# Row-wise argmax on one core: the last four tiles in column pieces, the last two looked up on VectorE, the last stored from its partitions

## The chip, the cores and the metric

The kernel runs on one core of one Trainium2 chip. The metric is device time in microseconds (us). All runs named here are of state fast, the granted clock was 1.00 in every profile, and nearly all executions of one kernel agree within about 0.1%. Engines: VectorE is DVE in the profile, GpSimd is POOL, ScalarE is ACT, TensorE is PE, SyncE is SP. A "q" behind a name (SPq, POOLq) marks what only that engine's sequencer does. In every profile the time of that execution is 1.8 us more than its span (the prediction reckons with 1.9, the difference of the median and the span).

## The reference

```python
def setup_inputs():
    return {"x": np.random.randn(8192, 8192).astype(np.float32)}

def reference(x):
    return np.argmax(x, axis=1)
```

## The kernel before

There are 64 tiles of 128 rows. Each row of 8192 numbers is 64 chunks of 128. A tile is loaded (4 MB), VectorE takes the maximum of each chunk (`cm`), and then the row's argmax is looked up in two steps: which chunk holds the row maximum (`k`), and where in that chunk it is (`k2`); for the second step the chunk is gathered again from DRAM with an indirect DMA that GpSimd issues. The matches (equal to the maximum, times a descending ramp) are on GpSimd. Lookups are made for groups of four tiles, and the three steps of a group are deferred so that they fall between the maxima of later tiles. Below, the *keys* of tiles are the VectorE step that reads `k` and so releases their gathers; their *finish* is the last step, which writes the result into `res`.

```python
    groups = [4] * 15 + [2, 1, 1]
    ...
    def store(t0, n):
        ps = ppool.tile([n, P], F32, tag="ps")
        nc.tensor.transpose(ps, res[:, t0:t0 + n], ident)
        o = spool.tile([n, P, 2], I32, tag="o")
        nc.gpsimd.memset(o, 0)
        nc.scalar.copy(out=o[:, :, 0:1], in_=ps.unsqueeze(2))
        keep(nc.sync.dma_start(out=out_i32[t0:t0 + n, :], in_=...))

    def stage2(t0, g, cm, now):
        mx = ...                                       # row maximum, VectorE
        w, k = first_match(cm, mx, descC, C, g, "c")   # GpSimd
        def stage3():
            keep(nc.vector.reduce_max(out=k, in_=w, axis=AX.X))
            ...                                        # idx, VectorE
            for i in range(g):
                keep(nc.gpsimd.indirect_dma_start(out=ga[:, i, :], ...))
            w2, k2 = first_match(ga, mx, descL, L, g, "l")   # GpSimd
            def stage4():
                ...                                    # three VectorE steps into res
                if t0 + g == 60:
                    store(0, 60)
            defer(now + 4, stage4)
        defer(now + 1, stage3)

    t = 0
    for g in groups:
        ...
        for i in range(g):
            ...
            parts = 4 if t == NT - 1 else 1            # the last tile in four pieces
            ...                                        # loads (SP queue), then maxima
            run_due(t)
            t += 1
        stage2(t0, g, cm, t - 1)
    run_due(0, all_=True)
    while pending:
        run_due(0, all_=True)
    store(60, NT - 60)
```

Of the kernel before, what the change touches and what calls it, by code (L numbers as in the profile page):

```python
# [1 line left out]

# [4 lines left out]

F32 = mybir.dt.float32
U32 = mybir.dt.uint32
I32 = mybir.dt.int32  # L10
ALU = mybir.AluOpType
AX = mybir.AxisListType


@with_exitstack
def kernel(
    ctx: ExitStack,
    tc: tile.TileContext,
    x: bass.AP,
    out: bass.AP,  # L20
):
    nc = tc.nc
    keep = tc.keep_in_program_order
    N, M = x.shape
    P = 128
    C = 64
    L = M // C
    NT = N // P

    xpool = ctx.enter_context(tc.tile_pool(name="x_sbuf", bufs=5))  # L30
    spool = ctx.enter_context(tc.tile_pool(name="small", bufs=3))
    cpool = ctx.enter_context(tc.tile_pool(name="const", bufs=1))
    ppool = ctx.enter_context(tc.tile_pool(name="psum", bufs=2, space=bass.MemoryType.PSUM))

    oth = out.tensor
    oth2 = type(oth)(name=oth.name, shape=[NT, 2 * P], dtype=I32, base_partition=oth.base_partition)
    out_i32 = oth2.ap()
    x_flat = x.tensor.reshape([N * C, L]).ap()


    descC = cpool.tile([P, C], F32)
    nc.gpsimd.iota(out=descC, pattern=[[-1, C]], base=C, channel_multiplier=0,  # L42
                   allow_small_or_imprecise_dtypes=True)
    descL = cpool.tile([P, L], F32)
    nc.gpsimd.iota(out=descL, pattern=[[-1, L]], base=L, channel_multiplier=0,  # L45
                   allow_small_or_imprecise_dtypes=True)

    base = cpool.tile([P, NT], F32)
    nc.gpsimd.iota(out=base, pattern=[[P * C, NT]], base=C, channel_multiplier=C,  # L49
                   allow_small_or_imprecise_dtypes=True)  # L50

    ident = cpool.tile([P, P], F32)
    nc.gpsimd.iota(out=ident, pattern=[[1, P]], base=0, channel_multiplier=-1,  # L53
                   allow_small_or_imprecise_dtypes=True)
    keep(nc.gpsimd.tensor_scalar(out=ident, in0=ident, scalar1=0.0, scalar2=None, op0=ALU.is_equal))  # L55

    res = cpool.tile([P, NT], F32)

    def first_match(vals, mx, desc, n, g, name):

        w = spool.tile([P, g, n], F32, tag=f"w_{name}")
        for i in range(g):
            keep(nc.gpsimd.tensor_scalar(out=w[:, i, :], in0=vals[:, i, :], scalar1=mx[:, i:i + 1],  # L63
                                    scalar2=None, op0=ALU.is_equal))
            keep(nc.gpsimd.tensor_tensor(out=w[:, i, :], in0=w[:, i, :], in1=desc, op=ALU.mult))  # L65
        k = spool.tile([P, g], F32, tag=f"k_{name}")
        return w, k

    groups = [4] * 15 + [2, 1, 1]
    assert sum(groups) == NT  # L70


    pending = []

    def run_due(now, all_=False):
        while pending and (all_ or pending[0][0] <= now):
            pending.pop(0)[1]()

    def defer(due, fn):
        pending.append((due, fn))  # L80
        pending.sort(key=lambda e: e[0])

    def store(t0, n):
        ps = ppool.tile([n, P], F32, tag="ps")
        nc.tensor.transpose(ps, res[:, t0:t0 + n], ident)  # L85
        o = spool.tile([n, P, 2], I32, tag="o")
        nc.gpsimd.memset(o, 0)  # L87
        nc.scalar.copy(out=o[:, :, 0:1], in_=ps.unsqueeze(2))  # L88
        keep(nc.sync.dma_start(out=out_i32[t0:t0 + n, :], in_=o.rearrange("t p two -> t (p two)")))

    def stage2(t0, g, cm, now):
        mx = spool.tile([P, g], F32, tag="mx")
        keep(nc.vector.reduce_max(out=mx, in_=cm, axis=AX.X))  # L93
        w, k = first_match(cm, mx, descC, C, g, "c")

        def stage3():
            keep(nc.vector.reduce_max(out=k, in_=w, axis=AX.X))  # L97
            idx = spool.tile([P, g], U32, tag="idx")
            keep(nc.vector.tensor_tensor(out=idx, in0=base[:, t0:t0 + g], in1=k, op=ALU.subtract))  # L99
            ga = spool.tile([P, g, L], F32, tag="ga")  # L100
            for i in range(g):
                keep(nc.gpsimd.indirect_dma_start(  # L102
                    out=ga[:, i, :], out_offset=None, in_=x_flat[:, :],
                    in_offset=bass.IndirectOffsetOnAxis(ap=idx[:, i:i + 1], axis=0)))
            w2, k2 = first_match(ga, mx, descL, L, g, "l")

            def stage4():
                keep(nc.vector.reduce_max(out=k2, in_=w2, axis=AX.X))  # L108

                keep(nc.vector.scalar_tensor_tensor(out=res[:, t0:t0 + g], in0=k, scalar=float(L),  # L110
                                               in1=k2, op0=ALU.mult, op1=ALU.add))
                keep(nc.vector.tensor_scalar(out=res[:, t0:t0 + g], in0=res[:, t0:t0 + g],  # L112
                                        scalar1=-1.0, scalar2=float(C * L + L),
                                        op0=ALU.mult, op1=ALU.add))
                if t0 + g == 60:
                    store(0, 60)

            defer(now + 4, stage4)

        defer(now + 1, stage3)  # L120

    t = 0
    for g in groups:
        cm = spool.tile([P, g, C], F32, tag="cm")
        t0 = t
        for i in range(g):
            xt = xpool.tile([P, M], F32, tag="xt")
            parts = 4 if t == NT - 1 else 1
            w = M // parts
            cw = C // parts  # L130
            for q in range(parts):
                keep(nc.sync.dma_start(out=xt[:, q * w:(q + 1) * w],  # L132
                                  in_=x[t * P:(t + 1) * P, q * w:(q + 1) * w]))
            for q in range(parts):
                keep(nc.vector.reduce_max(  # L135
                    out=cm[:, i, q * cw:(q + 1) * cw],
                    in_=xt[:, q * w:(q + 1) * w].rearrange("p (c l) -> p c l", c=cw), axis=AX.X))
            run_due(t)
            t += 1
        now = t - 1  # L140
        stage2(t0, g, cm, now)
    run_due(0, all_=True)
    while pending:
        run_due(0, all_=True)
    store(60, NT - 60)


# [1 line left out]
_INS = ['x']  # L149
_OUTS = [((8192,), 'int64')]  # L150


# [23 lines left out]
```

## Time and profile before

| | before |
|---|---|
| time, median of the rounds with the change | 667.21 us (667.04 to 667.47) |
| span of the profile | 665.3 us |
| VectorE busy, GpSimd busy | 584.1 us (88%), 179.7 us (27%) |
| last packet of the input (DMA records of the trace) | 639.76 us |
| end of tile 63's last maximum | 648.08 us |

The page of the kernel before, the span in 40 slices of 16.6 us; busy tenths, and GB/s moved.

```profile
DVE  2899898998989899898998989899898998989891
...
DMA  9999999999999999999999999999999999999930
GB/s 378 441 428 425 424 441 426 426 431 420 439 426 428 426 426 440 423 430 420 430 423 442 431 418 430 425 440 418 430 431 426 439 421 430 428 426 439 405 161 12
```

The DMA engines are full (9 tenths; 418 to 442 GB/s from the second slice to the 37th) up to the last two slices. The kernel is bound by the stream of its input for some 640 us; only what comes after can be saved by other work on the tail.

The timeline of the kernel before from 599 us on (start us, length us, engine, line, operation, tiles; in brackets the idle time before it and what ended it).

```profile
599.63 8.69 DVE L135 TENSOR_REDUCE cm<-xt 128x64 f32<-128x8192 f32 x1 [1.28 <-DMA xt<-in_x_dram]
...
609.55 8.68 DVE L135 TENSOR_REDUCE cm<-xt 128x64 f32<-128x8192 f32 x1
...
619.02 1.04 POOL L102 DMA_INDIRECT ga<-in_x_dram,idx  x1 [5.99 <-DVE idx L99]
619.05 8.69 DVE L135 TENSOR_REDUCE cm<-xt 128x64 f32<-128x8192 f32 x1 [0.31 <-DMA xt<-in_x_dram]
...
626.79 0.62 POOL L63 TENSOR_SCALAR w<-ga,mx 128x128 f32<-128x128 f32 x1 [2.97 <-DMA ga<-in_x_dram,idx]
...
630.11 8.69 DVE L135 TENSOR_REDUCE cm<-xt 128x64 f32<-128x8192 f32 x1 [2.05 <-DMA xt<-in_x_dram]
...
639.23 8.85 DVE L135 TENSOR_REDUCE cm<-xt 128x16 f32<-128x2048 f32 x4
...
649.93 1.05 POOL L102 DMA_INDIRECT ga<-in_x_dram,idx  x1 [4.57 <-DVE mx L93]
...
655.27 1.04 POOL L102 DMA_INDIRECT ga<-in_x_dram,idx  x1 [0.73 <-DVE idx L99]
...
658.70 0.45 POOL L65 TENSOR_TENSOR w<-w,descL 128x128 f32<-128x128 f32 x1
...
660.38 0.26 ACT L88 CAST o<-ps 4x128 int32<-4x128 f32 x1 [10.47 <-PE ps L85]
```

Tiles 59 to 63 are the five maxima. VectorE begins a whole tile only when all of it has landed (its waits of 1.28, 0.31 and 2.05 us above end with the landing), so it ends it at least 8.7 us after that: it runs about one tile behind the stream. After tile 63 (648.08) the gather of tile 62 (649.93) and the gather of tile 63 (655.27) stand one after the other.

### The profile page before, as it was taken

The page shows a single profiled execution, that of the slowest core. Times are in us where ns is not written, and L with a number is a line of the kernel's source. Part 1 is how long each engine was busy: PE and PEld are TensorE (multiplying, and loading weights), DVE is VectorE, ACT ScalarE, POOL GpSimd, SP SyncE. Part 2 cuts the span into 40 slices and gives each one's busy share as a digit, 9 for nine tenths or more (in the row PEclk, how much of TensorE's full clock was granted, in tenths as well). Part 3 has the DMA queues.
Part 4 walks back from the last instruction along what each step waited for, and adds up shares of the span by engine and source line. Part 5 has one row for each costly group of instructions (what it writes and reads, how often), then busy time and mean ns, then how long its engine had stood idle before and what let it go on. Part 6 is the DMA issues. An engine that isn't in the chain of part 4 may idle for free.

```text
span 665.3 us, 723 instructions
## 1 busy us (share of the span) xinstructions
PE 0.8 (0%) x2; PEld 0.2 (0%) x2; DVE 584.1 (88%) x175; ACT 1.8 (0%) x3; POOL 179.7 (27%) x331
## 2 busy tenths in 40 slices
PE   0000000000000000000000000000000000000000
PEld 0000000000000000000000000000000000000000
DVE  2899898998989899898998989899898998989891
ACT  0000000000000000000000000000000000000000
POOL 1004214041231304214032231304214131331442
DMA  9999999999999999999999999999999999999930
GB/s 378 441 428 425 424 441 426 426 431 420 439 426 428 426 426 440 423 430 420 430 423 442 431 418 430 425 440 418 430 431 426 439 421 430 428 426 439 405 161 12
DMA packets 11786, 272.75 MB, mean 410 GB/s; under 512 B 2116, under 2 KB 2180, under 8 KB 3204
## 3 DMA queue, kind: packets, MB, share of 16 engines
q1 hardware_dynamic: 9731, 268.51, 94.5%
q0 software_dynamic: 2048, 4.20, 1.7%
q14 instruction: 7, 0.05, 0.0%
HBM read 272.63 MB, written 0.07 MB: 410 GB/s over the span
## 4 chain that ended last, share of the span: by engine, by line
DMA 76%; DVE 19%; issue 3%; POOL 0%; SPq 0%; POOLq 0%; PE 0%; ACT 0%; DVEq 0%; ACTq 0%
DMA xt<-in_x_dram 75%; DVE cm L135 18%; DMA ga<-in_x_dram,idx 1%; DVE k L108 0%; SPq L132 0%; POOL w L63 0%; DVE mx L93 0%; DVE k L97 0%; DVE res L110 0%; POOL w L65 0%; DVE res L112 0%; POOLq L171 0%; DVE idx L99 0%; PE ps L85 0%; ACT o L88 0%
## 5 line engine op out<-in xcount | busy, mean ns | idle before, releaser
L135 DVE TENSOR_REDUCE cm<-xt 128x64 f32<-128x8192 f32 (+1 forms) x67 | 555.9, 8301 | 65.9 <-DMA xt<-in_x_dram 65.9
L63 POOL TENSOR_SCALAR w<-cm,mx 128x64 f32<-128x64 f32 x64 | 28.2, 441 | 261.4 <-DVE mx L93 261.4
L102 POOL DMA_INDIRECT ga<-in_x_dram,idx x64 | 62.4, 974 | 115.0 <-DVE idx L99 91.2
L63 POOL TENSOR_SCALAR w<-ga,mx 128x128 f32<-128x128 f32 x64 | 38.8, 606 | 91.7 <-DMA ga<-in_x_dram,idx 91.7
L65 POOL TENSOR_TENSOR w<-w,descL 128x128 f32<-128x128 f32 x64 | 29.1, 454 | 5.3
L65 POOL TENSOR_TENSOR w<-w,descC 128x64 f32<-128x64 f32 x64 | 20.4, 319 | 5.3
L108 DVE TENSOR_REDUCE k<-w 128x4 f32<-128x512 f32 (+2 forms) x18 | 11.1, 617 | 2.9 <-POOL w L65 2.9
L97 DVE TENSOR_REDUCE k<-w 128x4 f32<-128x256 f32 (+2 forms) x18 | 6.8, 379 | 4.8 <-POOL w L65 4.8
L93 DVE TENSOR_REDUCE mx<-cm 128x4 f32<-128x256 f32 (+2 forms) x18 | 6.9, 382 | 0.1
L99 DVE TENSOR_TENSOR idx<-base,k 128x4 uint32<-128x4 f32 (+2 forms) x18 | 2.9, 162 | 0.9 <-DVE k L97 0.3
L112 DVE TENSOR_SCALAR res<-res 128x4 f32<-128x4 f32 (+2 forms) x18 | 3.0, 168 | 0.6
L110 DVE SCALAR_TENSOR_TENSOR res<-k 128x4 f32<-128x4 f32 (+2 forms) x18 | 2.9, 162 | 0.6
L88 ACT CAST o<-ps 60x128 int32<-60x128 f32 (+1 forms) x2 | 0.5, 263 | 658.1 <-PE ps L85 658.1
L85 PE MATMUL ps<-ident,res 128*60 128x128 f32 (+1 forms) x2 | 0.8, 382 | 659.5 <-DVE k L97 649.2
L88 ACT ACT_TABLE_LOAD x1 | 1.3, 1283 | 0.7 <-PEq L160 0.7
L87 POOL MEMSET o<- 60x256 int32 (+1 forms) x2 | 0.6, 301 | 0.0
L55 POOL TENSOR_SCALAR ident<-ident 128x128 f32<-128x128 f32 x1 | 0.5, 534 | 0.0
L85 PEld LDWEIGHTS ps<-ident,res 128*60 128x60 f32 (+1 forms) x2 | 0.2, 104 | 659.8 <-issue 649.2
L42 POOL IOTA descC<- 128x64 f32 x1 | 0.2, 175 | 0.4 <-POOLq L160 0.4
L45 POOL IOTA descL<- 128x128 f32 x1 | 0.2, 228 | 0.0
L53 POOL IOTA ident<- 128x128 f32 x1 | 0.2, 228 | 0.0
L49 POOL IOTA base<- 128x64 f32 x1 | 0.2, 174 | 0.0
(4 smaller groups left out, 0.4 us busy)
## 6 DMA issues: line engine op xcount, KB each, us to landing
xt<-in_x_dram SPq DMA_DIRECT2D x63, 4096.0 KB, 41.0
xt<-in_x_dram SPq DMA_DIRECT2D x4, 1024.0 KB, 37.5
ga<-in_x_dram,idx POOLq DMA_INDIRECT x64, 8.6
out_dram<-o SPq DMA_DIRECT2D x1, 60.0 KB, 1.6
out_dram<-o SPq DMA_DIRECT2D x1, 4.0 KB
```

The lines of the kernel that those rows point to most:

```text
L63: keep(nc.gpsimd.tensor_scalar(out=w[:, i, :], in0=vals[:, i, :], scalar1=mx[:, i:i + 1], scalar2=None, op0=ALU.is_equal))
L65: keep(nc.gpsimd.tensor_tensor(out=w[:, i, :], in0=w[:, i, :], in1=desc, op=ALU.mult))
L85: nc.tensor.transpose(ps, res[:, t0:t0 + n], ident)
L88: nc.scalar.copy(out=o[:, :, 0:1], in_=ps.unsqueeze(2))
L93: keep(nc.vector.reduce_max(out=mx, in_=cm, axis=AX.X))
L97: keep(nc.vector.reduce_max(out=k, in_=w, axis=AX.X))
L99: keep(nc.vector.tensor_tensor(out=idx, in0=base[:, t0:t0 + g], in1=k, op=ALU.subtract))
L102: keep(nc.gpsimd.indirect_dma_start(out=ga[:, i, :], out_offset=None, in_=x_flat[:, :], in_offset=bass.IndirectOffsetOnAxis(ap=idx[:, i:i ...
L108: keep(nc.vector.reduce_max(out=k2, in_=w2, axis=AX.X))
L110: keep(nc.vector.scalar_tensor_tensor(out=res[:, t0:t0 + g], in0=k, scalar=float(L), in1=k2, op0=ALU.mult, op1=ALU.add))
L112: keep(nc.vector.tensor_scalar(out=res[:, t0:t0 + g], in0=res[:, t0:t0 + g], scalar1=-1.0, scalar2=float(C * L + L), op0=ALU.mult, op1=ALU ...
L135: keep(nc.vector.reduce_max(out=cm[:, i, q * cw:(q + 1) * cw], in_=xt[:, q * w:(q + 1) * w].rearrange("p (c l) -> p c l", c=cw), axis=AX.X))
```

## The change

The intent is to shorten the tail: tiles 60 to 63 are loaded and maximized in pieces, so that VectorE can follow the stream; the deferred lookups are counted in pieces, so that they fall between them; tiles 62 and 63 are looked up by VectorE's own max and index instructions, without GpSimd's matches; and tile 63's result goes to DRAM from its 128 partitions, 8 bytes each, without transpose and copy. The first store moves to ScalarE's queue, and the groups' finish comes one tile earlier. The diff, cut to its core:

```diff
-    groups = [4] * 15 + [2, 1, 1]
+    def load_reduce(t, cm, widths):
+        ...                                  # one load per piece, then one maximum per piece
+            step[0] = t * 4 + at // 2048
+            run_due()
...
     def store(t0, n):
...
-        keep(nc.sync.dma_start(out=out_i32[t0:t0 + n, :], ...))
+        keep(nc.scalar.dma_start(out=out_rows[t0:t0 + n, :], ...))
...
-            defer(now + 4, stage4)
-        defer(now + 1, stage3)
+            defer(match_after, finish)
+        defer(gather_after, gather)
+
+    def direct_begin(t, cm):
+        keep(nc.vector.max(out=m8, in_=cm))
+        keep(nc.vector.max_index(out=c8, in_max=m8, in_values=cm))
+        keep(nc.vector.tensor_tensor(out=idx, in0=c8[:, 0:1], in1=base[:, t:t + 1], op=ALU.add))
+        keep(nc.gpsimd.indirect_dma_start(out=ga, ...))
+        return m8, c8, ga
+
+    def direct_end(m8, c8, ga, dst):
+        keep(nc.vector.max_index(out=l8, in_max=m8, in_values=ga))
+        keep(nc.vector.scalar_tensor_tensor(out=dst, in0=c8[:, 0:1], scalar=float(L), ...))
...
+    for g in [4] * 15 + [2]:
...
+            load_reduce(t, cm[:, i, :], [M] if t < 60 else [2048] * 4)
...
+        if g == 4:
+            lookup(t0, g, cm, 4, 7)
+        else:
+            lookup(t0, g, cm, 1, 100)
+
+    load_reduce(62, cm62, [2048] * 4)
+    d62 = direct_begin(62, cm62)
+    load_reduce(63, cm63, [2048] * 3 + [1024, 512, 512])
+    d63 = direct_begin(63, cm63)
+    step[0] = 1000
+    run_due()
+    direct_end(*d62, res[:, 62:63])
+    store(60, 3)
+    direct_end(*d63, o_last[:, 0:1])
+    nc.sync.dma_start(out=out_pairs[63 * P:, :], in_=o_last)
```

More of the change, by code (lines that the diff above doesn't have):

```diff
@@ L35, with out_view @@
     oth = out.tensor
-    oth2 = type(oth)(name=oth.name, shape=[NT, 2 * P], dtype=I32, base_partition=oth.base_partition)
-    out_i32 = oth2.ap()
+    def out_view(shape):
+        return type(oth)(name=oth.name, shape=shape, dtype=I32, base_partition=oth.base_partition).ap()
+    out_rows = out_view([NT, 2 * P])
+    out_pairs = out_view([N, 2])
     x_flat = x.tensor.reshape([N * C, L]).ap()
@@ L48 @@
     base = cpool.tile([P, NT], F32)
-    nc.gpsimd.iota(out=base, pattern=[[P * C, NT]], base=C, channel_multiplier=C,
+    nc.gpsimd.iota(out=base, pattern=[[P * C, NT]], base=0, channel_multiplier=C,
+                   allow_small_or_imprecise_dtypes=True)
+    baseC = cpool.tile([P, NT], F32)
+    nc.gpsimd.iota(out=baseC, pattern=[[P * C, NT]], base=C, channel_multiplier=C,
                    allow_small_or_imprecise_dtypes=True)
@@ L57, with defer, run_due, match @@
     res = cpool.tile([P, NT], F32)
-    def first_match(vals, mx, desc, n, g, name):
-        w = spool.tile([P, g, n], F32, tag=f"w_{name}")
+    o_last = cpool.tile([P, 2], I32)
+    nc.gpsimd.memset(o_last, 0)
+    pending = []
+    step = [0]
+    def defer(steps, fn):
+        pending.append((step[0] + steps, fn))
+        pending.sort(key=lambda e: e[0])
+    def run_due():
+        while pending and pending[0][0] <= step[0]:
+            pending.pop(0)[1]()
+    def load_reduce(t, cm, widths):
+        assert sum(widths) == M
+        xt = xpool.tile([P, M], F32, tag="xt")
+        at = 0
+        for w in widths:
+            keep(nc.sync.dma_start(out=xt[:, at:at + w], in_=x[t * P:(t + 1) * P, at:at + w]))
+            at += w
+        at = 0
+        for w in widths:
+            c0, c1 = at // L, (at + w) // L
+            keep(nc.vector.reduce_max(
+                out=cm[:, c0:c1], in_=xt[:, at:at + w].rearrange("p (c l) -> p c l", l=L), axis=AX.X))
+            at += w
+            step[0] = t * 4 + at // 2048
+            run_due()
+    def match(w, vals, mx, desc, g):
         for i in range(g):
             keep(nc.gpsimd.tensor_scalar(out=w[:, i, :], in0=vals[:, i, :], scalar1=mx[:, i:i + 1],
-                                    scalar2=None, op0=ALU.is_equal))
+                                         scalar2=None, op0=ALU.is_equal))
             keep(nc.gpsimd.tensor_tensor(out=w[:, i, :], in0=w[:, i, :], in1=desc, op=ALU.mult))
-        k = spool.tile([P, g], F32, tag=f"k_{name}")
-        return w, k
-    groups = [4] * 15 + [2, 1, 1]
-    assert sum(groups) == NT
-    pending = []
-    def run_due(now, all_=False):
-        while pending and (all_ or pending[0][0] <= now):
-            pending.pop(0)[1]()
-    def defer(due, fn):
-        pending.append((due, fn))
-        pending.sort(key=lambda e: e[0])
     def store(t0, n):
@@ L85, in store, with lookup, gather @@
         nc.tensor.transpose(ps, res[:, t0:t0 + n], ident)
-        o = spool.tile([n, P, 2], I32, tag="o")
+        o = cpool.tile([n, P, 2], I32, tag=f"o{t0}")
         nc.gpsimd.memset(o, 0)
-        nc.scalar.copy(out=o[:, :, 0:1], in_=ps.unsqueeze(2))
-        keep(nc.sync.dma_start(out=out_i32[t0:t0 + n, :], in_=o.rearrange("t p two -> t (p two)")))
-    def stage2(t0, g, cm, now):
+        keep(nc.scalar.copy(out=o[:, :, 0:1], in_=ps.unsqueeze(2)))
+        keep(nc.scalar.dma_start(out=out_rows[t0:t0 + n, :], in_=o.rearrange("t p two -> t (p two)")))
+    def lookup(t0, g, cm, gather_after, match_after):
         mx = spool.tile([P, g], F32, tag="mx")
         keep(nc.vector.reduce_max(out=mx, in_=cm, axis=AX.X))
-        w, k = first_match(cm, mx, descC, C, g, "c")
-        def stage3():
-            keep(nc.vector.reduce_max(out=k, in_=w, axis=AX.X))
+        wc = spool.tile([P, g, C], F32, tag="wc")
+        match(wc, cm, mx, descC, g)
+        k = spool.tile([P, g], F32, tag="k")
+        def gather():
+            keep(nc.vector.reduce_max(out=k, in_=wc, axis=AX.X))
             idx = spool.tile([P, g], U32, tag="idx")
-            keep(nc.vector.tensor_tensor(out=idx, in0=base[:, t0:t0 + g], in1=k, op=ALU.subtract))
+            keep(nc.vector.tensor_tensor(out=idx, in0=baseC[:, t0:t0 + g], in1=k, op=ALU.subtract))
             ga = spool.tile([P, g, L], F32, tag="ga")
@@ L104, in stage3 @@
                     in_offset=bass.IndirectOffsetOnAxis(ap=idx[:, i:i + 1], axis=0)))
-            w2, k2 = first_match(ga, mx, descL, L, g, "l")
-            def stage4():
-                keep(nc.vector.reduce_max(out=k2, in_=w2, axis=AX.X))
-                keep(nc.vector.scalar_tensor_tensor(out=res[:, t0:t0 + g], in0=k, scalar=float(L),
-                                               in1=k2, op0=ALU.mult, op1=ALU.add))
-                keep(nc.vector.tensor_scalar(out=res[:, t0:t0 + g], in0=res[:, t0:t0 + g],
-                                        scalar1=-1.0, scalar2=float(C * L + L),
-                                        op0=ALU.mult, op1=ALU.add))
+            wl = spool.tile([P, g, L], F32, tag="wl")
@@ new lines, in gather, with finish @@
+            match(wl, ga, mx, descL, g)
+            def finish():
+                k2 = spool.tile([P, g], F32, tag="k2")
+                keep(nc.vector.reduce_max(out=k2, in_=wl, axis=AX.X))
+                r = res[:, t0:t0 + g]
+                keep(nc.vector.scalar_tensor_tensor(out=r, in0=k, scalar=float(L), in1=k2,
+                                                    op0=ALU.mult, op1=ALU.add))
+                keep(nc.vector.tensor_scalar(out=r, in0=r, scalar1=-1.0, scalar2=float(C * L + L),
+                                             op0=ALU.mult, op1=ALU.add))
@@ L115, in stage4 @@
                 if t0 + g == 60:
                     store(0, 60)
-            defer(now + 4, stage4)
-        defer(now + 1, stage3)
+            defer(match_after, finish)
+        defer(gather_after, gather)
+    def direct_begin(t, cm):
+        m8 = spool.tile([P, 8], F32, tag="m8")
+        keep(nc.vector.max(out=m8, in_=cm))
+        c8 = spool.tile([P, 8], U32, tag="c8")
+        keep(nc.vector.max_index(out=c8, in_max=m8, in_values=cm))
+        idx = spool.tile([P, 1], U32, tag="idx1")
+        keep(nc.vector.tensor_tensor(out=idx, in0=c8[:, 0:1], in1=base[:, t:t + 1], op=ALU.add))
+        ga = spool.tile([P, L], F32, tag="ga1")
+        keep(nc.gpsimd.indirect_dma_start(
+            out=ga, out_offset=None, in_=x_flat[:, :],
+            in_offset=bass.IndirectOffsetOnAxis(ap=idx[:, :1], axis=0)))
+        return m8, c8, ga
@@ L122 @@
+    def direct_end(m8, c8, ga, dst):
+        l8 = spool.tile([P, 8], U32, tag="l8")
+        keep(nc.vector.max_index(out=l8, in_max=m8, in_values=ga))
+        keep(nc.vector.scalar_tensor_tensor(out=dst, in0=c8[:, 0:1], scalar=float(L), in1=l8[:, 0:1],
+                                            op0=ALU.mult, op1=ALU.add))
     t = 0
-    for g in groups:
+    for g in [4] * 15 + [2]:
         cm = spool.tile([P, g, C], F32, tag="cm")
@@ L126 @@
         for i in range(g):
-            xt = xpool.tile([P, M], F32, tag="xt")
-            parts = 4 if t == NT - 1 else 1
-            w = M // parts
-            cw = C // parts
-            for q in range(parts):
-                keep(nc.sync.dma_start(out=xt[:, q * w:(q + 1) * w],
-                                  in_=x[t * P:(t + 1) * P, q * w:(q + 1) * w]))
-            for q in range(parts):
-                keep(nc.vector.reduce_max(
-                    out=cm[:, i, q * cw:(q + 1) * cw],
-                    in_=xt[:, q * w:(q + 1) * w].rearrange("p (c l) -> p c l", c=cw), axis=AX.X))
-            run_due(t)
-            t += 1
-        now = t - 1
-        stage2(t0, g, cm, now)
-    run_due(0, all_=True)
-    while pending:
-        run_due(0, all_=True)
-    store(60, NT - 60)
+            load_reduce(t, cm[:, i, :], [M] if t < 60 else [2048] * 4)
+            t += 1
+        if g == 4:
+            lookup(t0, g, cm, 4, 7)
+        else:
+            lookup(t0, g, cm, 1, 100)
+    cm62 = spool.tile([P, C], F32, tag="cm1")
+    load_reduce(62, cm62, [2048] * 4)
+    d62 = direct_begin(62, cm62)
+    cm63 = spool.tile([P, C], F32, tag="cm1")
+    load_reduce(63, cm63, [2048] * 3 + [1024, 512, 512])
[6 more added lines that the diff above has]
+    nc.sync.dma_start(out=out_pairs[63 * P:, :], in_=o_last)
 _INS = ['x']
```

## The prediction

> **What bounds it now.** The page's slices show the DMA engines full (9 tenths, 420-440 GB/s) to about 632 us; the stretches put the input stream's end near 638-640. Until there the kernel is bound by the stream, whose bytes and first 60 tiles the change leaves alone. The rest (to 665.3) is tail. In the timeline VectorE (DVE) maximizes tile 62 only from 630.11 and tile 63 from 639.23 to 648.08; then the chain of waits is serial: old results 1.0, gather of tile 62 2.55, GpSimd (POOL) matches 2.0, gather of tile 63 2.64, POOL match and DVE steps 2.0, transpose and copy 0.7, and 4.6 from the last copy (660.64) to the span's end.
>
> **What the change does.**
> 1. Pieces for tiles 60-62. DVE runs about one tile (8.7) behind the stream, without a wait before tiles 60 and 63, so it does not reach the stream's end. Only its waits before tiles 61 (0.31) and 62 (2.05) go, 2.4 in all. Tile 63's four pieces took 8.85 against 8.69, so pieces cost about 0.15 a tile.
> 2. Old lookups (finish of group 56-59, 1.0; keys of 60-61, 0.45) move from behind tile 63 in between pieces; 62's new lookup (estimate 0.75) does as well. Tile 63 should then end on DVE at about 646.8, not 648.1.
> 3. After it: estimate 0.75 (max, max_index, index add), one gather 2.64 + 0.3 to start, 0.6 (max_index, multiply-add), then the store from 128 partitions, 4.6[...]. That replaces 17.2 by about 9.3. The finish of 60-61 and the store of 60-62 hide under the gather.
>
> Sum: span about 656, time = span + 1.9 = 658 (the profiled run before: 667.03 for 665.3).
>
> **Risk in the middle.** DVE's order puts the keys of 60-61 after the first piece of tile 62 (about 629.1). They need POOL's match for 60-61, which stands behind four gathers of 56-59. Before, those issued from 619.02, the first match started at 626.79, and POOL was done at 634.3. With the same landings DVE would stall about 4 and the time would be about 662. I expect less: the gathers share the 16 DMA engines with the stream, whose rows are now 8 KB instead of 32 KB. [...] gathers took 8.6 to land (median of the DMA issues), and the two at 639-641, with the stream drained, about 2.6. Whether short rows alone bring this no run shows yet. I give 65% to gathers of about 4 and little stall, 30% to a stall of 3-4.5.
>
> **Not worth time:** SP's 18 issues (0.33 to 0.5 each, 40 ahead); extra iota and memsets; earlier finishing of the main groups. The stream may end 1 later (8 KB packets 314 ns, a quarter of 1218: 3% slower over three tiles), but DVE comes to the last pieces only at 644.
>
> **Checks.** Stream end 639-642. No DVE wait on xt from tile 60 on. Tile 63's last piece ends 645.5-648 (650-651.5 if stalled). One gather of 2.6-3 in the last chain, no POOL match there, no PE or ACT. Last DVE instruction to span's end 4.6-5.5. Tile 63's last piece to the end 9-10, was 17.2.
>
> **What would make it wrong:** the stall (line k waiting on POOL wc); 8-byte stores landing slowly; max_index far above 0.35; a DVE that catches up with the stream.
>
> Predicted 658.7, range 656.3 to 662.5; faster by over 2% (below 654.0) 0.03, within 2% 0.96, slower 0.01.

The sum was 646.8 for the end of tile 63's last piece plus 9.3 after it: a span of 656, a time of 658. One was a term of the 9.3, beside the 4.6 of the last store; the terms that are left there come to 8.9 (0.75 + 2.64 + 0.3 + 0.6 + 4.6). For gathers of about 4, the 4 is no more than the author's estimate, between the 8.6 and the 2.6 of the trace (measured in the changed kernel: 5.9 to the first match). The 0.75, the 0.6 and the 0.35 of a max_index were estimates too, from before any trace here held these instructions; the changed kernel's trace shows 0.78, 0.58 and 0.30 to 0.37 (point 3 below).

## More of the kernel before

The instructions at the end of the program, in the view of the line that holds them (durations in ns as minimum, median, maximum, then first and last start in us).

```profile
L171 POOLq DRAIN  x3: 40/102/5810, 658.7 to 665.0; - x3
L171 SPq DRAIN  x3: 7/7/7, 662.2 to 664.7; - x3
```

The reader should keep the 5810 ns in mind: GpSimd's first drain starts at 658.66, just before its last real instruction, and ends at 664.47, 5.32 us after that instruction's end (659.15). SP, which waits for the store, was through with its waits at 662.2. The timeline counts no drains, and the chain of waits ends with ScalarE's copy and shows only 0.50 us of this one, so neither shows it.

## The result

| | before | changed |
|---|---|---|
| time, median | 667.21 us | 659.16 us (659.07 to 659.45) |
| span | 665.3 us | 657.3 us |
| last packet of the input | 639.76 us | 640.92 us |
| end of tile 63's last maximum | 648.08 us | 648.80 us |
| end of GpSimd's last instruction | 659.15 us | 650.79 us |

The ratio is 0.988 (95% interval 0.9863 to 0.9897), clear of noise. Ratios are the mean time of one kernel's fast runs over that of the other's in the same rounds, so not quite the ratio of the medians that are quoted.

The page of the changed kernel, the same lines.

```profile
DVE  2899898998989989898998989989899998989986
...
DMA  9999999999999999999999999999999999999990
GB/s 383 431 431 439 415 439 425 421 439 430 423 431 425 428 434 423 427 439 418 436 423 427 440 423 425 426 431 433 429 425 425 439 423 429 433 421 416 420 371 9
```

The stream is as full as before; its end only moves against a shorter span.

The timeline of the changed kernel.

```profile
608.57 8.85 DVE L92 TENSOR_REDUCE cm<-xt 128x16 f32<-128x2048 f32 x4
...
617.86 8.86 DVE L92 TENSOR_REDUCE cm<-xt 128x16 f32<-128x2048 f32 x4
618.23 1.04 POOL L127 DMA_INDIRECT ga<-in_x_dram,idx  x1 [6.17 <-DVE idx L124]
...
624.10 0.62 POOL L101 TENSOR_SCALAR wl<-ga,mx 128x128 f32<-128x128 f32 x1 [1.08 <-DMA ga<-in_x_dram,idx]
...
631.07 0.28 DVE L122 TENSOR_REDUCE k<-wc 128x2 f32<-128x128 f32 x1 [1.83 <-POOL wc L103]
...
639.82 8.98 DVE L92 TENSOR_REDUCE cm<-xt 128x16 f32<-128x2048 f32 x6
...
649.42 0.16 DVE L156 TENSOR_TENSOR idx<-c,base 128x1 uint32<-128x1 uint32 x1
...
649.85 0.94 POOL L158 DMA_INDIRECT ga<-in_x_dram,idx  x1 [8.27 <-DVE idx L156]
...
652.41 0.09 DVE L165 MATCH_VALUE_LOAD l<-m,ga 128x8 f32 x1 [1.64 <-DMA ga<-in_x_dram,idx]
...
652.81 0.16 DVE L166 SCALAR_TENSOR_TENSOR o_last<-c,l 128x1 int32<-128x1 uint32 x1
653.03 0.35 SPq L192 DMA_DIRECT2D out_dram<-o_last  x1
```

VectorE has no wait for the stream from tile 60 on, and one wait of 1.83 us for GpSimd at the keys of tiles 60 and 61. Tile 63 starts at 639.82, as late as before, and ends 0.7 later than before. But the index for its gather is there 0.8 us after that, and one gather and two VectorE steps finish the row.

The end of the program, changed kernel.

```profile
L218 POOLq DRAIN  x3: 40/102/6470, 649.6 to 657.0; - x3
...
L218 SPq DRAIN  x3: 7/7/7, 656.5 to 656.8; - x3
```

GpSimd's drain starts at 649.63 and ends at 656.10, again 5.30 us after GpSimd's last instruction, which is now the issue of tile 63's gather (649.85 + 0.94 = 650.79). SP, which waits for the 8-byte store, is later here (656.47), by 0.37.

### The profile page after: what moved, and what is told of

Its sections match the earlier page's. It is cut to its first block, busy times and chain, and to the rows that moved or that the text cites. A ratio compares the mean times of both kernels' runs of the same rounds, so it can differ in the third digit from the quotient of the medians.

```text
span 657.3 us, 739 instructions
## 1 busy us (share of the span) xinstructions
PE 0.8 (0%) x2; PEld 0.2 (0%) x2; DVE 587.6 (89%) x188; ACT 1.8 (0%) x3; POOL 175.9 (27%) x325
## 4 chain that ended last, share of the span: by engine, by line
DMA 78%; DVE 16%; issue 4%; POOL 1%; SPq 0%; POOLq 0%; DVEq 0%
DMA xt<-in_x_dram 76%; DVE cm L92 15%; DMA ga<-in_x_dram,idx 2%; POOL ga L127 0%; POOL wl L101 0%; SPq L87 0%; POOL wl L103 0%; POOL ga L158 0%; DVE k L122 0%; POOL wc L101 0%; POOL wc L103 0%; DVE mx L116 0%; DVE l L165 0%; DVE idx L124 0%; POOLq L218 0%
## 5 line engine op out<-in xcount | busy, mean ns | idle before, releaser
L92 DVE TENSOR_REDUCE cm<-xt 128x64 f32<-128x8192 f32 (+2 forms) x78 | 556.9, 7152 | 59.4 <-DMA xt<-in_x_dram 59.4
L101 POOL TENSOR_SCALAR wc<-cm,mx 128x64 f32<-128x64 f32 x62 | 27.3, 440 | 249.2 <-DVE mx L116 249.2
L101 POOL TENSOR_SCALAR wl<-ga,mx 128x128 f32<-128x128 f32 x62 | 37.5, 605 | 92.0 <-DMA ga<-in_x_dram,idx 92.0
L103 POOL TENSOR_TENSOR wl<-wl,descL 128x128 f32<-128x128 f32 x62 | 28.1, 453 | 5.2
L103 POOL TENSOR_TENSOR wc<-wc,descC 128x64 f32<-128x64 f32 x62 | 19.7, 318 | 5.2
L135 DVE TENSOR_REDUCE k<-wl 128x4 f32<-128x512 f32 (+1 forms) x16 | 10.5, 659 | 0.0
L122 DVE TENSOR_REDUCE k<-wc 128x4 f32<-128x256 f32 (+1 forms) x16 | 6.4, 401 | 1.8 <-POOL wc L103 1.8
L116 DVE TENSOR_REDUCE mx<-cm 128x4 f32<-128x256 f32 (+1 forms) x16 | 6.6, 412 | 0.6
L140 DVE TENSOR_SCALAR res<-res 128x4 f32<-128x4 f32 (+1 forms) x16 | 2.7, 170 | 0.5
L124 DVE TENSOR_TENSOR idx<-baseC,k 128x4 uint32<-128x4 f32 (+1 forms) x16 | 2.6, 162 | 0.6
```

Of the source, the lines that this page charges most:

```text
L92: keep(nc.vector.reduce_max(out=cm[:, c0:c1], in_=xt[:, at:at + w].rearrange("p (c l) -> p c l", l=L), axis=AX.X))
L101: keep(nc.gpsimd.tensor_scalar(out=w[:, i, :], in0=vals[:, i, :], scalar1=mx[:, i:i + 1], scalar2=None, op0=ALU.is_equal))
L103: keep(nc.gpsimd.tensor_tensor(out=w[:, i, :], in0=w[:, i, :], in1=desc, op=ALU.mult))
L116: keep(nc.vector.reduce_max(out=mx, in_=cm, axis=AX.X))
L122: keep(nc.vector.reduce_max(out=k, in_=wc, axis=AX.X))
L124: keep(nc.vector.tensor_tensor(out=idx, in0=baseC[:, t0:t0 + g], in1=k, op=ALU.subtract))
```

## The experiments

All times are medians of 5 rounds. The medians of the kernel before in the three sets of rounds were 667.04 (a to d), 667.22 (e to h) and 667.22 (i to l). Each set ran on another chip, and the changed kernel was not run again in them, so a difference from its 659.16 carries some 0.2 us between sets; for the small differences of b, c and g the traces count more than the times. All kernels gave the right result. The short diffs are against the changed kernel, except where they say "kernel before".

### a_keys_later

```diff
-            lookup(t0, g, cm, 1, 100)
+            lookup(t0, g, cm, 2, 100)
```

> Changed kernel, keys of tiles 60-61 taken on VectorE after the second piece of tile 62 instead of the first. Theory (VectorE's one-tile lag sets the tail, and its 1.83 us wait for GpSimd is pure loss): the wait goes, tile 63's last piece ends about 1.8 earlier (647.0 instead of 648.8 from the span's start), time 657.3. Rival (the stream sets the tail, or the wait only moves to tile 63's pieces or to the gather of 62): time within 0.5 of the changed kernel's 659.2.

657.43 us, ratio 0.9855. There is no wait at the keys (they start at 631.60, right after the second piece), and tile 63's last piece ends at 647.13. Timeline:

```profile
631.60 0.27 DVE L122 TENSOR_REDUCE k<-wc 128x2 f32<-128x128 f32 x1
...
638.15 8.98 DVE L92 TENSOR_REDUCE cm<-xt 128x16 f32<-128x2048 f32 x6
```

The wait was pure loss on VectorE, as the theory has it, and the stream did not take its place.

### b_whole_60_62

```diff
-            load_reduce(t, cm[:, i, :], [M] if t < 60 else [2048] * 4)
+            load_reduce(t, cm[:, i, :], [M])
...
-    load_reduce(62, cm62, [2048] * 4)
+    load_reduce(62, cm62, [M])
```

> Changed kernel, tiles 60 to 62 loaded and maximized whole again, tile 63 in its six pieces, all lookups as changed. Theory (VectorE starts the tail a whole tile behind, so pieces of three tiles buy only VectorE's waits for tiles 61 and 62): waits of about 1 before 61 and up to 2 before 62 return, the key stall of 1.8 goes since keys now follow all of tile 62: tile 63's last piece ends about 650, time about 660.3 (+1.1). Gathers of tiles 56-59 again start their first match about 7.7 after their first issue (5.9 with pieces). Rival (the pieces are the main gain of the 8 us): 663 or more.

659.80 us, ratio 0.9892. Timeline of this run:

```profile
619.00 8.69 DVE L92 TENSOR_REDUCE cm<-xt 128x64 f32<-128x8192 f32 x1 [0.50 <-DMA xt<-in_x_dram]
...
626.72 0.62 POOL L101 TENSOR_SCALAR wl<-ga,mx 128x128 f32<-128x128 f32 x1 [3.15 <-DMA ga<-in_x_dram,idx]
...
630.06 8.69 DVE L92 TENSOR_REDUCE cm<-xt 128x64 f32<-128x8192 f32 x1 [2.06 <-DMA xt<-in_x_dram]
```

The waits of VectorE are back (0.50 before tile 61, 2.06 before 62), and the time rises by only 0.6. But the wait of 1.83 at the keys is gone as well, since the keys now follow all of tile 62. So 0.6 is what the pieces were worth net of the wait that came with them; against run a, which has the pieces and no such wait, run b is 2.4 slower, about the two waits together. More they could not save: at that point VectorE is already a tile behind.

### c_store_transposed

```diff
-    store(60, 3)
-    direct_end(*d63, o_last[:, 0:1])
-    nc.sync.dma_start(out=out_pairs[63 * P:, :], in_=o_last)
+    direct_end(*d63, res[:, 63:64])
+    store(60, 4)
```

> Changed kernel, tile 63 stored with 60-62 through the transpose and ScalarE's queue. Theory: transpose and copy of about 0.75 come into the last chain, the write itself takes about the same: time about 660.0 (+0.8 to +1.0). Rival (128 rows of 8 bytes land slower than 4 rows of 1 KB by as much as the transpose costs): 659.2, no difference.

658.68 us, ratio 0.9875: not slower, but about 0.5 us faster than the changed kernel. Both expectations missed. The timeline and, below it, the end of the program:

```profile
652.76 0.16 DVE L166 SCALAR_TENSOR_TENSOR res<-c,l 128x1 f32<-128x1 uint32 x1
...
653.45 0.26 ACT L110 CAST o<-ps 4x128 int32<-4x128 f32 x1 [15.72 <-PE ps L107]
653.74 0.26 ACTq L111 DMA_DIRECT2D out_dram<-o  x1
```

```profile
L217 POOLq DRAIN  x3: 40/102/6470, 649.6 to 656.6; - x3
L217 SPq DRAIN  x3: 7/7/7, 655.0 to 656.3; - x3
```

The transpose and copy are in the chain (0.78 us from VectorE's last end to ACT's last end), and yet SP is through with its waits at 655.06, 1.4 earlier than in the changed kernel: by the landing records of the trace, the 4 rows of 1 KB had landed 1.23 us after the start of their issue, the 128 rows of 8 bytes only after 2.92. The queue is not the reason: the last store of the kernel before, also 4 rows of 1 KB but on SP's queue, had landed after 1.24. Nor do the packets take long: those of 8 bytes took 9 ns each (median) and were all over 1.04 us after the start of the issue, those of 1 KB 0.91; the difference lies between the last packet and the landing (1.88 against 0.32). The span then ends with GpSimd's drain (656.05), not with the store.

### d_pool_lookup

```diff
-    d62 = direct_begin(62, cm62)
+    lookup(62, 1, cm62, 2, 100)
...
-    d63 = direct_begin(63, cm63)
+    lookup(63, 1, cm63, 0, 1000, o_last[:, 0:1])   # last step writes o_last
...
```

> Changed kernel, pieces and stores as changed, but tiles 62 and 63 looked up with GpSimd matches as the others are, tile 62's keys after the second piece of tile 63. Theory: the chain after tile 63's last piece gets two GpSimd matches (0.85 and 1.1 with their starts) and more VectorE steps, about 6.6 instead of 4.2 to the last VectorE instruction; time about 661.5 (+2.4). Rival (the direct lookup matters mainly because it keeps GpSimd's queue out of the end, so tile 63's chain would also wait for 62's matches): 663 or more.

662.14 us, ratio 0.9926, so +3.0 instead of +2.4. The chain from tile 63's last piece (648.49) to the last VectorE instruction (654.91) takes 6.4 us instead of 4.2, as expected. The size is off because that chain is not what ends the span: GpSimd's last instruction is now the match, which ends at 654.22, 3.42 later than the gather's issue in the changed kernel; less the 0.37 by which the changed kernel's store is later than its drain, and 0.02 for the two fixed parts (the drain is 0.02 longer, the rest after it 0.04 shorter than after SP), that is the 3.0.

### e_before_order

```diff
 # kernel before, in the loop over the pieces of the last tile
+                if parts > 1 and q == 1:
+                    run_due(t)
```

> Kernel before, only the order changed: what is due (finish of tiles 56-59, keys of tile 62) runs on VectorE after tile 63's second piece instead of after its fourth. Theory (a good part of the old 17.2 us tail was tile 62's lookup standing in front of tile 63's): tile 63's last piece ends about 2.2 later (650.3, with a stall of 0.8 for GpSimd), tile 63's gather starts about 3 earlier (652.3 instead of 655.27), time about 664.2 (-3.0). Rival (order is worth nothing without the direct lookup): 667.

664.43 us, ratio 0.9956, 2.8 us less than before with nothing but the order changed (3.0 was expected). Tile 63's maxima end later, at 650.90, and its gather starts earlier, at 652.82 instead of 655.27, because the gather of tile 62 no longer stands in front of it:

```profile
646.42 4.48 DVE L135 TENSOR_REDUCE cm<-xt 128x16 f32<-128x2048 f32 x2 [0.21 <-issue]
646.49 1.05 POOL L102 DMA_INDIRECT ga<-in_x_dram,idx  x1 [0.73 <-DVE idx L99]
...
652.82 1.04 POOL L102 DMA_INDIRECT ga<-in_x_dram,idx  x1 [0.73 <-DVE idx L99]
```

### f_pieces_from_48

```diff
-            load_reduce(t, cm[:, i, :], [M] if t < 60 else [2048] * 4)
+            load_reduce(t, cm[:, i, :], [M] if t < 48 else [2048] * 4)
```

> Changed kernel, pieces of 2048 columns from tile 48 on instead of from 60. Theory (VectorE is a tile behind because it may start a tile only when it has landed whole; with about 0.7 us of slack a tile it catches up with the stream over 12 tiles): stream ends about 3.6 later than in the changed kernel (8 KB rows), about 644.8, but tile 63's last piece ends within 1.5 of the stream's end, about 646 instead of 648.8; time about 656.4 (-2.8). Rival (VectorE's work, not its lag, sets the tail; more pieces only slow the stream): 659 to 663.

657.02 us, ratio 0.9848. The stream ends at 644.11, 3.2 later than in the changed kernel, and tile 63's last piece ends at 646.48, 2.4 after the stream (1.5 was expected) and 2.3 earlier than in the changed kernel. Timeline, an early and a late piece:

```profile
549.20 2.29 DVE L92 TENSOR_REDUCE cm<-xt 128x16 f32<-128x2048 f32 x1 [0.20 <-DMA xt<-in_x_dram]
...
626.36 2.29 DVE L92 TENSOR_REDUCE cm<-xt 128x16 f32<-128x2048 f32 x1 [0.28 <-DMA xt<-in_x_dram]
```

From 549.20 on, VectorE waits for single pieces: it has caught up within about seven tiles. In the changed kernel VectorE's waits for four whole tiles (from 549.78 on: 1.69, 0.28, 0.58 and 0.50) come to 0.76 a tile, against the 0.7 of slack expected. The lag of one tile was the cause of the late tile 63, and pieces cure it, if they begin early enough. They have a price: the more tiles come in 8 KB rows, the later the stream ends (640.92 with tiles from 60 on, 642.12 from 56 in run l, 643.16 from 53 in run k, 644.11 from 48 here), and a packet of 8 KB took 314 ns against 304.5 for a quarter of one of 32 KB.

### g_pieces_1024

```diff
-... [M] if t < 60 else [2048] * 4
+... [M] if t < 60 else [1024] * 8
-    load_reduce(62, cm62, [2048] * 4)
+    load_reduce(62, cm62, [1024] * 8)
```

> Changed kernel, tiles 60-62 in eight pieces of 1024 columns (4 KB rows). It asks what a gather waits for in the stream. If a fixed number of the stream's rows stands ahead of each gather: first match of tiles 56-59 about 4 after its first issue, no stall at the keys of 60-61, time about 658. If a fixed number of bytes: first match about 5.9 after the first issue as with 8 KB rows, stall of about 1.8 again, time about 659.8.

658.79 us, ratio 0.9873; the wait at the keys is 0.97, but only because VectorE comes to them 0.8 later; they start at 631.02, against 631.07 in the changed kernel. The gathers of tiles 56 to 59, by the row size of the stream that they share the DMA engines with (times after the first gather's issue; the middle two columns from the DMA and landing records of the trace):

| run, row size | first packet starts | landed | first match starts |
|---|---|---|---|
| before, 32 KB | 4.12 | 7.67 | 7.76 |
| b, 32 KB | 4.30 | 7.86 | 7.95 |
| changed, 8 KB | 4.42 | 5.78 | 5.87 |
| g, 4 KB | 4.30 | 5.57 | 5.66 |

So neither guess of ours is the whole of it. Shorter rows did not bring the first packet of the first gather sooner: it waited 4.1 to 4.4 us with any row size, which speaks against a fixed number of rows ahead of it. What they shortened there is the time from the first packet to the landing, 3.6 with 32 KB rows and 1.4 and 1.3 with 8 and 4 KB. The other three gathers did gain before their first packet: it started 5.4 to 5.9 after their issue with 32 KB rows and 4.2 to 4.3 with shorter ones. Of these times 1.65 to 1.76 are there without the stream (the last gather of each of these runs). What the rest consists of is left open.

### h_before_finish3

```diff
 # kernel before
-            defer(now + 4, stage4)
+            defer(now + 3, stage4)
```

> Kernel before, only the groups' finish moved one tile earlier, as the change does for the main groups. Theory (the first 60 tiles are bound by the stream): no difference, 667.0 within 0.7; if anything 0.7 less at the end, since the finish of tiles 56-59 no longer stands after tile 63. Rival (evener VectorE work frees buffers earlier and speeds the stream): 2 or more less, with the stream's end earlier.

674.13 us, ratio 1.0104: 6.9 us slower, which neither theory had. Timeline:

```profile
640.48 0.42 SPq L89 DMA_DIRECT2D out_dram<-o  x1
641.00 2.00 SPq L132 DMA_DIRECT2D xt<-in_x_dram  x4
...
646.17 2.29 DVE L135 TENSOR_REDUCE cm<-xt 128x16 f32<-128x2048 f32 x1 [6.04 <-DMA xt<-in_x_dram]
```

With the earlier finish, the first store stands in SP's program in front of tile 63's four loads. SP waits for the store's data until 640.5, and only then issues loads that in the kernel before went out some 37 us before they landed.

### j_finish3_act

```diff
 # kernel before, with the edit of h and
-        keep(nc.sync.dma_start(out=out_i32[t0:t0 + n, :], ...))
+        keep(nc.scalar.dma_start(out=out_i32[t0:t0 + n, :], ...))
```

> Kernel before, the groups' finish one tile earlier as in h_before_finish3, and both stores issued from ScalarE's queue instead of SP's. Theory (h lost 7 us because the first store stood in SP's program ahead of tile 63's loads, which were issued only at 641.0): those loads go out early again, time 666.9 within 0.7, like the kernel before. Rival (the earlier finish itself hurts, by VectorE waiting for GpSimd): 670 or more.

666.83 us, ratio 0.9995. That is the reading of h confirmed. On the kernel before, the earlier finish and the store on ScalarE's queue together save nothing, but without the move of the store the earlier finish costs 7 us. The changed kernel with the store on SP's queue was not run.

### i_late_pool

```diff
     direct_end(*d63, o_last[:, 0:1])
+    scratch = cpool.tile([P, 2], I32)
+    keep(nc.gpsimd.tensor_copy(out=scratch, in_=o_last))
```

> Changed kernel plus one useless GpSimd copy of 128x2 that must wait for the last VectorE result. All traces so far show a drain on GpSimd at the end of the program that ends 5.30 to 5.32 after GpSimd's last instruction, in the kernel before (659.15 to 664.47) as in the changed one (650.80 to 656.10), whatever the store does. Theory (that drain, and not the store, set the end of the kernel before and is within 0.45 of doing so now): the copy ends about 653.2, the drain about 658.5, the span grows by about 2.0 to 659.3, time about 661.2. Rival (the store sets the end, the drain only waits along with it): 659.2, no difference.

661.31 us, ratio 0.991, 2.15 more than the changed kernel. The timeline and the end of the program:

```profile
653.25 0.18 POOL L193 COPY scratch<-o_last 128x2 int32<-128x2 int32 x1 [2.27 <-DVE o_last L166]
```

```profile
L220 POOLq DRAIN  x3: 40/102/5523, 653.2 to 659.3; - x3
L220 SPq DRAIN  x3: 7/7/7, 656.6 to 659.0; - x3
```

A copy of 0.18 us that nothing needs makes the kernel 2 us longer. The drain ends at 658.75, 5.32 after the copy, while SP is through at 656.65, much as in the changed kernel (656.47). So the end of the span is the later of two things: SP's waits for the stores, and GpSimd's last instruction plus 5.3 us; then another 0.8. The traces of the kernel before, of the changed kernel and of all twelve runs fit within 0.05 us; seven of them:

| run | GpSimd's last instruction ends | its drain ends | SP through | span |
|---|---|---|---|---|
| before | 659.15 | 664.47 | 662.18 | 665.26 |
| changed | 650.79 | 656.10 | 656.47 | 657.29 |
| c | 650.75 | 656.05 | 655.06 | 656.84 |
| d | 654.22 | 659.53 | 658.73 | 660.32 |
| e | 656.64 | 661.96 | 659.66 | 662.74 |
| i | 653.44 | 658.75 | 656.65 | 659.54 |
| l | 646.73 | 652.03 | 651.26 | 652.81 |

The columns are from the instruction records of each trace. The drain takes the same 5.30 to 5.32 after a gather's issue, a multiply and a copy; what it waits for, the records do not show.

### k_from_53 and l_from_56

```diff
-... [M] if t < 60 else [2048] * 4          # k: t < 53, l: t < 56
-            lookup(t0, g, cm, 4, 7)
+            lookup(t0, g, cm, 4, 7 if t < 60 else 100)   # finish of 56-59 after the last gather
-            lookup(t0, g, cm, 1, 100)
+            lookup(t0, g, cm, 2, 100)
 # and the store of run c
```

> Candidate: changed kernel with pieces of 2048 columns from tile 53 on, keys of 60-61 after the second piece of tile 62, finish of 56-59 moved behind the last gather, and tile 63 stored through the transpose (4 rows, ScalarE's queue). Theory (the end is set by when GpSimd issues the last gather, plus 5.3 of drain and 0.8): last gather issued by about 646.2, against 650.8 in the changed kernel and 648.5 with pieces from 48; span about 652.3, time about 654.2. If moving the finish only trades places with a wait: 655.2.

> As k_from_53 but pieces from tile 56 on. The stream is about 0.9 shorter (three tiles fewer in 8 KB rows), but VectorE has four tiles fewer to catch up in. If VectorE has caught up by tile 61 all the same: 653.3. If it has not: 654.5 or more, with no wait of VectorE for the stream after tile 60.

k took 655.58 us, ratio 0.9824; l took 654.58 us, ratio 0.9812 (95% interval 0.9799 to 0.9825, so it stays unclear whether it passes the threshold of 2%), the fastest of all, 1.9% below the kernel before and 0.7% below the changed one. k missed its 654.2 and came near its other case, 655.2: the last gather was out only at 647.77, 1.6 later than expected. VectorE had caught up and waited for single pieces from tile 58 on, last for two of tile 63's (0.15 and 0.27): the stream, which ends at 643.16, takes the bound back. l fell between its two cases: VectorE caught up, but only at tile 62. The timeline of l:

```profile
627.19 2.29 DVE L92 TENSOR_REDUCE cm<-xt 128x16 f32<-128x2048 f32 x1 [0.42 <-DMA xt<-in_x_dram]
...
640.12 4.60 DVE L92 TENSOR_REDUCE cm<-xt 128x16 f32<-128x2048 f32 x4 [0.25 <-DMA xt<-in_x_dram]
...
645.78 0.95 POOL L158 DMA_INDIRECT ga<-in_x_dram,idx  x1 [6.24 <-DVE idx L156]
```

In l VectorE waits for pieces of tile 63 until 640.12, so up to there the stream bounds it again; the stream ends at 642.12 (k: 643.16), 2.6 us before tile 63's last maximum ends (644.72). After that come the lookup, the last gather's issue and the fixed end.

## Why the prediction was right or wrong, point by point

The predicted time, 658.7, is 0.5 below the measured 659.16. The reasons were not all right.

1. **"DVE runs about one tile behind the stream, so it does not reach the stream's end": right.** No wait for the stream from tile 60 on; tile 63 began at 639.82 against 639.23 before. Runs a and b show that the pieces of 60 to 62 are worth about the waits they remove (2.4 us; 0.6 with the new wait of point 2), run f that VectorE catches up when they begin earlier. The stream's end was 640.92, within the 639 to 642 given.
2. **"Tile 63 should then end on DVE at about 646.8": wrong, it was 648.80,** outside 645.5 to 648. The term that failed is "gathers of about 4 and little stall": the first match came 5.9 us after the first issue, not 4, and VectorE waited 1.83 for GpSimd. Taking that wait away (run a) brought 647.13. The risk had been named, and its two branches had been weighed; the truth lay between them. That the gathers take longer beside the stream the trace shows (first packet 4.1 us and more after the issue, 1.65 to 1.76 without it), but the shorter rows took less off their way than the prediction gave: 7.8 us from the first issue to the first match became 5.9, not 4 (table at g). The reason that the prediction gave for the 4 is cut; by what mechanism gathers and stream share the engines was not shown.
3. **"0.75, one gather 2.64 + 0.3 to start, 0.6": right.** Measured 0.78 to the end of the index (649.58), 0.27 to the gather's issue, 2.54 to its landing in the chain of waits, and 0.58 to the end of the last VectorE instruction (652.97). By instruction: for 128x64, max 0.23, value load 0.09 and index search 0.22; for 128x128 the search took 0.28. The direct lookup takes GpSimd's matches out of the end; undoing it costs 3.0 us (run d).
4. **"Then the store from 128 partitions, 4.6": wrong in its cause, and too long.** Measured 4.33 from VectorE's last instruction to the span's end. The 4.6 between the last copy and the end of the kernel before was taken for the store's. It was GpSimd's drain: the kernel before ended 5.32 us after GpSimd's last match, plus 0.8, and its store had been done more than 2 us before that. Hence leaving out the transpose and copy could save nothing, and the 8-byte rows cost about 0.5 (run c). The checks "last DVE instruction to span's end 4.6-5.5" and "tile 63's last piece to the end 9-10" (8.50) failed with it.
5. **The size of the gain.** By the drain's account it is exact: GpSimd's last instruction ends 8.36 us earlier (659.15 to 650.79), the end is set 0.38 later by the 8-byte store, and the two fixed parts together are 0.02 longer: 7.96, the difference of the spans. About 3 of it belongs to the direct lookup (run d), the order of the old lookups alone is worth 2.8 in the kernel before (run e), the pieces of 60 to 62 about 0.6 net of the wait that they brought (run b). These were taken from different kernels and do not simply add.
6. **Why it landed so near.** The sum of the terms gave a span of 656; tile 63 came 2.0 later than that and the end 0.7 earlier, which gives 657.3. The quoted 658.7 stands 0.7 above the sum of 658, which can be read as a hedge for the wait, though the prediction does not say so; and the step from span to time was 0.1 too long. Errors of opposite sign and a hedge made it close: that the number fits so well is luck.

## What to carry to other kernels

Ask how late each engine's last instruction is, not only the chain of the result: here GpSimd held the end of the program for 5.3 us after its last, even useless, instruction. Cutting the last loads into pieces helped here as far as the consumer had time left to catch up (from tile 60 on VectorE did not, from 48 it had within about seven tiles), so try to begin several tiles ahead, but no earlier than needed, since shorter rows slowed the stream (3.2 us for twelve more tiles in run f). And look where a store stands in the issuing engine's program: in front of loads, it held them back here (6.9 us in run h).
